# A hybrid decoder step on one core: part of the weight residuals computed on GpSimd, with seven part buffers and five raw buffers

## The chip, the cores and the metric

The kernel runs on one core of a Trainium2 chip. The metric is the device time of one execution in microseconds (us); several executions are timed and the median is given. A core has TensorE (PE in the profile, its weight loads PEld), VectorE (DVE), ScalarE (ACT), GpSimd (POOL) and SyncE (SP, which here only issues the loads of the weights).

## The reference: what is computed

One decoder layer on 264 tokens (256 of a new sequence and 8 single-token samples), all in float32, cut to what matters here:

```
h = h + 0.5 * swiglu(rmsnorm(h), ffn1_gate, ffn1_up, ffn1_down)
h = h + mixing_block(rmsnorm(h), w_in, ..., w_out)     # mLSTM heads beside short gated convolutions
h = h + 0.5 * swiglu(rmsnorm(h), ffn2_gate, ffn2_up, ffn2_down)
y = rmsnorm(h)

def swiglu(x, wg, wu, wd):
    return (jax.nn.silu(x @ wg) * (x @ wu)) @ wd
```

The model width is 2048 and the feed-forward width 5504, so that gate, up and down are 2048 x 5504 matrices, twice. They are read once, and each of their 128x128 blocks meets all 264 tokens.

## The kernel before, in words

**Two parts for each number.** TensorE multiplies float16 here. Each float32 weight tile, scaled by sw = 2^14, is cut into a high part hi = f16(sw*w) and a low part lo = f16(sw*w - hi), and the activations likewise; a product is hi*xhi + hi*xlo + lo*xhi, three matmuls (`three`, L324 to L327).

**One weight tile's way.** `fetch` (L257) takes the next tile from a fixed list (`weight_plan`, L93). A tile is 128 partitions by up to 8 blocks of 128 columns, 512 KB: a quarter of a gate-and-up block's weights. It is loaded into a raw buffer (wraw, six of them, AHEAD + 1) by a transfer that SP issues (L264); ScalarE writes the high part into a part buffer (w, also six), in `high` (L243); VectorE writes the low part with one scalar_tensor_tensor, sw*raw - hi, in `low` (L251). `release` (L285) issues the low parts. While the flag lag is set, as it is in the feed-forward stages from the fourth (first layer) or second (second layer) block on, the low part of a tile is issued one fetch after its high part, so that it stands later in VectorE's row. A raw buffer is free again when the low part has been written, a part buffer when TensorE has used it.

**What sets the order.** The order on each engine is the order in which the code issues. `product` (L329) and `product_pair` (L364) fetch as long as fewer than AHEAD = 5 tiles are ready, so a tile's three instructions stand five tiles before its use, between the steps of whatever product is being issued then. `at` and `tick` (L310, L313) put the steps that follow a product (activation, joins) half a product or more behind it. Each engine works off its own row strictly in order and waits on semaphores.

**Two kinds of products.** A plain block of gate or up (`block`, L833) is two `product`s, gate and up, of 16 weight blocks each: four tiles. Some pairs of blocks go by `by_seven` (L815) instead: gate and up of one block are computed together by seven half-size products in place of eight. For that VectorE forms sums of weight parts (`weight_sums`, L299, four additions for two tiles, tiles named s), and afterwards joins three PSUM banks (`join`, L423, lines L430 to L440, tile y). In each feed-forward layer the blocks 0 to 21 make up the first half and 22 to 42 the second, each followed by the down products of that half. From block 7 on (first layer) or block 3 on (second layer) every second block goes by seven, up to 19 in the first half, and from 22 every second up to 40 in the second: 7, 10, 9 and 10 blocks in four stretches, with a plain block between any two. Blocks 20, 21, 41 and 42 are plain. In the down products of a half three to five of the eight pairs of output blocks go by seven.

**The steps around a plain block.** For the gate product: L840 multiplies the PSUM bank by the token's norm (tile ta), ScalarE takes a sum over a few tokens (L573, seen) and the SiLU (L843, tb). For up: L846 (tile tc), L789 (silu times up, tc), then high and low part of the activation (a, L243 and L251). For a block by seven: L430 on ScalarE, L433 to L440 and L821 on VectorE (y), L824 (SiLU, tb), L789 (y) and the parts a.

**GpSimd's work before.** In the feed-forward stages it has work only where h gets its final value: a square (L725) and a sum (L729) for each of the next norm's 16 blocks, and one addition near the start (L744).

Of the kernel before, what the change touches and what calls it, by code (L numbers as in the profile page):

```python
# [8 lines left out]
F32 = mybir.dt.float32  # L9
# [4 lines left out]
ALU = mybir.AluOpType  # L14
# [14 lines left out]
WK = 8  # L29
# [138 lines left out]
def step(ctx: ExitStack, tc: tile.TileContext, a: dict, shared, bad=None):  # L168
# [3 lines left out]
    half_size = bad is not None  # L172
    PART = F16 if half_size else F32R
    sw, sx, s3 = (SW, SX, S3) if half_size else (1.0, 1.0, 1.0)
    sa = SA if half_size else {"1": 1.0, "2": 1.0}
    AHEAD = 5 if half_size else 2
    queue = nc.gpsimd if half_size else nc.sync
    side = nc.gpsimd if half_size else nc.vector

# [3 lines left out]
    wpool = ctx.enter_context(tc.tile_pool(name="wpool", bufs=3))  # L183
# [56 lines left out]
    def high(dst, src, scale=1.0):  # L240

        if half_size or not isinstance(scale, float):
            nc.scalar.activation(dst, src, AF.Copy, scale=scale)  # L243
        else:
            nc.scalar.copy(dst, src)

    def low(dst, src, hi, scale=1.0):

        hi = hi if half_size else hi.bitcast(F32)
        if half_size or not isinstance(scale, float):  # L250
            nc.vector.scalar_tensor_tensor(  # L251
                dst, src, scale, hi, op0=ALU.mult, op1=ALU.subtract
            )
        else:
            nc.vector.tensor_tensor(dst, src, hi, op=ALU.subtract)

    def fetch():  # L257

        if not plan:
            return  # L260
        key, src, n, m, several = plan.pop(0)
        raw = wpool.tile([128, WK, 128], F32, tag="wraw", name="wraw", bufs=AHEAD + 1)[:, :n, :m]
        dst = raw.rearrange("p (f k) m -> p f k m", f=several) if several > 1 else raw
        nc.sync.dma_start(dst, src)  # L264
        parts = wpool.tile([128, 2, WK, 128], PART, tag="w", name="w", bufs=AHEAD + 1)
        hi, lo = parts[:, 0], parts[:, 1]
        pairs = [(raw, (hi, lo), slice(0, m))]
        if half_size and key == "gates":

            pairs = [(raw[:, :, 32 * g :], (hi, lo), slice(16 * g, 16 * g + 16)) for g in (0, 1)]  # L270
        lows = []
        for src, (h_, l_), cols in pairs:
            h_, l_ = h_[:, :n, cols], l_[:, :n, cols]
            src = src[:, :, : cols.stop - cols.start]
            high(h_, src, sw)
            lows.append((l_, src, h_, sw))
        release()
        held.append((lows, (key, hi, lo, n), parts))
        if not lag[0]:
            release()  # L280


    held, lag = [], [False]

    def release():  # L285
        for lows, tile_, parts in held:
            for x in lows:
                low(*x)
            ready.append(tile_)
            if tile_[0][1] in ("gu", "dd"):  # L290
                beside.append(parts)
                if len(beside) == 2:
                    sums.append(weight_sums(*beside, tile_[3] // 2))
                    beside.clear()
        held.clear()

    beside, sums, spool = [], [], [None]

    def weight_sums(one, other, n):  # L299

        s = spool[0].tile([128, 4, 2, WK // 2, 128], PART, tag="s", name="s", bufs=3)[:, :, :, :n]
        a_, b_, c_, d_ = (w[:, :, i : 2 * n : 2] for w in (one, other) for i in (0, 1))
        for out, x, y in ((0, c_, d_), (1, b_, d_), (2, s[:, 0], b_), (3, s[:, 2], a_)):
            nc.vector.tensor_tensor(s[:, out], x, y, op=ALU.add)  # L304
        return s
# [23 lines left out]
    def product(key, x, order, m=128):  # L329

        tick()
        ps = bank()[:m, :T]
        k, half = 0, 0.5
        while k < len(order):
            while plan and len(ready) + len(held) < AHEAD:
                fetch()
            got, hi, lo, n = ready.pop(0)
            assert got == key, (got, key)
            for i in range(n):
                three(  # L340
                    ps, hi[:, i, :m], lo[:, i, :m], x[order[k]], k == 0, k == len(order) - 1
                )
                k += 1
            if k < len(order) or lag[0]:
                fetch()
            tick(half)
            half = 0
        return ps
# [15 lines left out]
    def product_pair(key, x, forms, order):  # L364
# [12 lines left out]
        while k0 < count:  # L377
            tiles = []
            for _ in range(2):
                while plan and len(ready) + len(held) < AHEAD or not ready:  # L380
                    fetch()
                tiles.append(ready.pop(0))
                assert tiles[-1][0] == key, (tiles[-1][0], key)
# [63 lines left out]
    def product_beside(key, x):  # L447
# [3 lines left out]
        for k0 in range(0, KB, WK):  # L451
            while plan and len(ready) + len(held) < AHEAD:
                fetch()
# [14 lines left out]
    def products2(keys, x, order):  # L468
# [3 lines left out]
        while k < len(order):  # L472
            tick()
            for j, key in enumerate(keys):
                while plan and len(ready) + len(held) < AHEAD:
                    fetch()
# [1237 lines left out]
```

## Time and profile before

| what | value |
|---|---|
| three timed runs | 1808.15, 1808.59, 1811.59 us; median 1808.59 us |
| the profiled execution: its own time | 1812.5 us |
| its span, first to last instruction | 1810.7 us |
| TensorE busy, clock granted | 1784.7 us (99%), 0.996 |
| VectorE busy | 1572.0 us (87%) |
| ScalarE busy | 896.0 us (49%) |
| GpSimd busy | 145.9 us (8%) |
| low parts of weight tiles on VectorE (L251, tile w) | 692 instructions, 800.3 us |
| high parts of weight tiles on ScalarE (L243, tile w) | 692 instructions, 665.3 us |
| transfers, mean rate | 211 GB/s |

The page of the profile lists busy time, a picture of the span in 40 slices, the chain of work that ended last, and groups of instructions with the idle time before them and what ended it. A timeline row has the start, the duration (from the first start to the last end, where it stands for several instructions in a row), engine, line, operation, tiles and count; in square brackets stands the idle time ahead of it and what ended that. Durations of consecutive instructions of one engine overlap a little, since the next starts before the last writes of the one before have landed; so the distance of two starts is the better price. A table of windows gives, for a stretch of the span, each engine's busy time and count.

### The profile page before, as it was taken

How to read it: one execution, taken by the hardware profiler on the slowest of the kernel's cores; microseconds unless marked ns; L12 is line 12 of the kernel's file. 1: busy time of each engine (PE TensorE's matmuls, PEld its weight loads, DVE VectorE, ACT ScalarE, POOL GpSimd, SP SyncE). 2: the span in 40 equal slices, each digit the busy share in tenths (PEclk: the TensorE clock that was granted, in tenths of full speed). 3: DMA queues.
4: the chain of work that ended last, by engine and by line, in shares of the span. 5: the costliest groups of instructions: out<-in, count | busy, mean ns of one | idle time of the engine just before them, and what ended most of it. 6: DMA issues, size and time to landing. Idle time of an engine off the chain costs nothing.

```text
span 1810.7 us, 45495 instructions
## 1 busy us (share of the span) xinstructions
PE 1784.7 (99%) x19080; PEld 1595.9 (88%) x19080; DVE 1572.0 (87%) x2528; ACT 896.0 (49%) x1571; POOL 145.9 (8%) x200
## 2 busy tenths in 40 slices
PE   8999999999999999999999999999999999999997
PEld 7899889999898988888888888899989999898896
DVE  7889988999998998788888866999989999999895
ACT  7544444435445445576576744454454444444543
POOL 0000000000000222222121032000000000000131
PEclk9999999999999999999999999999999999999998
DMA  8656666666666556888787655666665656666663
GB/s 289 203 180 196 196 210 204 209 205 195 193 209 210 179 171 214 289 296 283 271 266 255 224 185 177 205 199 191 206 217 190 212 188 205 193 210 190 212 187 116
DMA packets 118518, 381.54 MB, mean 211 GB/s; under 512 B 14972, under 2 KB 24796, under 8 KB 118304
## 3 DMA queue, kind: packets, MB, share of 16 engines
q1 hardware_dynamic: 109104, 350.53, 60.2%
q0 software_dynamic: 8256, 27.57, 4.4%
q8 instruction: 151, 2.47, 0.5%
q10 hardware_dynamic: 944, 0.45, 0.1%
q14 instruction: 63, 0.52, 0.1%
HBM read 366.72 MB, written 11.78 MB: 209 GB/s over the span
## 4 chain that ended last, share of the span: by engine, by line
PE 74%; DVE 17%; ACT 4%; issue 3%; DMA 1%; SPq 0%; ACTq 0%; DVEq 0%
PE ps L327 17%; PE ps L325 17%; PE ps L326 17%; PE ps L390 8%; PE ps L374 7%; PE ps L375 7%; DVE w L251 6%; DVE s L304 5%; ACT w L243 3%; DMA wraw<-in_w1gu 1%; DVE g L362 1%; DVE a L251 1%; DVE y L821 1%; PE ps L682 0%; DVE y L434 0%
## 5 line engine op out<-in xcount | busy, mean ns | idle before, releaser
L251 DVE SCALAR_TENSOR_TENSOR w<-wraw,w 128x1024 f16<-128x1024 f32 (+3 forms) x692 | 800.3, 1182 | 100.2 <-ACT w L243 99.1
L243 ACT ACTIVATE w<-wraw 128x1024 f16<-128x1024 f32 (+3 forms) x692 | 665.3, 1007 | 150.3 <-issue 56.0
L327 PE MATMUL ps<-x,w 128*128 128x264 f16 x1536 | 424.9, 277 | 4.6 <-DVE w L251 4.6
L325 PE MATMUL ps<-x,w 128*128 128x264 f16 x1536 | 424.9, 277 | 0.0
L326 PE MATMUL ps<-x,w 128*128 128x264 f16 x1536 | 424.8, 277 | 0.0
L327 PEld LDWEIGHTS <-w 128*128 128x128 f16 x3372 | 330.2, 98 | 56.9 <-DVE w L251 8.5
L326 PEld LDWEIGHTS <-w 128*128 128x128 f16 x3372 | 330.2, 98 | 49.7
L325 PEld LDWEIGHTS <-w 128*128 128x128 f16 x3372 | 330.4, 98 | 48.4 <-issue 0.6
L325 PE MATMUL ps<-xm,w 128*128 128x264 f16 x896 | 247.4, 276 | 0.0
L326 PE MATMUL ps<-xm,w 128*128 128x264 f16 x896 | 247.4, 276 | 0.0
L327 PE MATMUL ps<-xm,w 128*128 128x264 f16 x896 | 247.4, 276 | 0.0
L390 PEld LDWEIGHTS <-w 128*128 128x128 f16 x1886 | 181.1, 98 | 27.0 <-ACT w L243 1.8
L374 PEld LDWEIGHTS <-s 128*128 128x128 f16 x1872 | 180.0, 96 | 2.3 <-DVE s L304 2.2
L375 PEld LDWEIGHTS <-s 128*128 128x128 f16 x1872 | 181.7, 97 | 0.0
L327 PE MATMUL ps<-a,w 128*128 128x264 f16 (+2 forms) x684 | 180.2, 269 | 1.4 <-DVE w L251 1.4
L325 PE MATMUL ps<-a,w 128*128 128x264 f16 (+2 forms) x684 | 180.2, 269 | 0.0
L326 PE MATMUL ps<-a,w 128*128 128x264 f16 (+2 forms) x684 | 180.2, 269 | 0.0
L304 DVE TENSOR_TENSOR s<-s,w 128x1024 f16<-128x1024 f16 (+2 forms) x246 | 164.8, 670 | 4.3
L304 DVE TENSOR_TENSOR s<-w 128x1024 f16<-128x1024 f16 (+2 forms) x246 | 156.5, 677 | 5.3
L390 PE MATMUL ps<-x,w 128*128 128x264 f16 x1152 | 141.8, 276 | 1.1 <-ACT w L243 1.1
L375 PEld LDWEIGHTS <-w 128*128 128x128 f16 x1418 | 138.3, 98 | 2.5 <-DVE w L251 0.4
L374 PEld LDWEIGHTS <-w 128*128 128x128 f16 x1418 | 138.1, 97 | 2.0
(273 smaller groups left out, 2296.8 us busy)
## 6 DMA issues: line engine op xcount, KB each, us to landing
wraw<-in_w2gu SPq DMA_DIRECT2D x172, 512.0 KB, 4.7
wraw<-in_w1gu SPq DMA_DIRECT2D x164, 512.0 KB, 4.5
wraw<-in_win SPq DMA_DIRECT2D x112, 512.0 KB, 5.4
wraw<-in_w1d SPq DMA_DIRECT2D x42, 512.0 KB, 4.5
wraw<-in_w2d SPq DMA_DIRECT2D x38, 512.0 KB, 4.4
wraw<-in_w2d SPq DMA_DIRECT2D x42, 448.0 KB, 4.2
wraw<-in_wout SPq DMA_DIRECT2D x32, 512.0 KB, 4.4
wraw<-in_w1d SPq DMA_DIRECT2D x36, 448.0 KB, 4.0
```

What stands on the lines that cost most here:

```text
L243: nc.scalar.activation(dst, src, AF.Copy, scale=scale)
L251: nc.vector.scalar_tensor_tensor(dst, src, scale, hi, op0=ALU.mult, op1=ALU.subtract)
L304: nc.vector.tensor_tensor(s[:, out], x, y, op=ALU.add)
L325: nc.tensor.matmul(ps, wh, xk[:, 0, :], start=first, stop=False)
L326: nc.tensor.matmul(ps, wh, xk[:, 1, :], start=False, stop=False)
L327: nc.tensor.matmul(ps, wl, xk[:, 0, :], start=False, stop=last)
L362: nc.vector.tensor_tensor(out[:, n], a_, b_, op=op)
L374: nc.tensor.matmul(ps, w[0], x[:, 1], start=first, stop=False)
L375: nc.tensor.matmul(ps, w[1], x[:, 0], start=False, stop=last)
L390: nc.tensor.matmul(ps[:, :T], hi[:, i], xs[i][:, 0], start=(k0 + i == 0), stop=False)
L821: nc.vector.tensor_tensor(z, z, norm.r.unsqueeze(1).to_broadcast([128, 2, T]), op=ALU.mult)
```

## The change

It has two parts.

**Buffers.** AHEAD goes from 5 to 6. With AHEAD + 1 part buffers there are seven, and tiles are fetched one tile earlier in the row. The raw buffers go from AHEAD + 1 = 6 to AHEAD - 1 = 5.

**Low parts on GpSimd.** The tiles of plain gate and up products and of plain down products of the first half are counted, and every second one is `apart`: ScalarE first writes the high part as before, then scales the raw tile in place (a second activation, raw times sw, float32 to float32), and the low part is a tensor_tensor subtraction on GpSimd, raw - hi, in place of VectorE's scalar_tensor_tensor. This concerns 114 of 692 tiles, 102 of 128x1024 and 12 of 128x896. In a plain gate-and-up block it is the second tile of gate and the second of up; in the down products of the first halves 18 tiles in all.

```diff
-    AHEAD = 5 if half_size else 2
+    AHEAD = 6 if half_size else 2
...
-        raw = wpool.tile([128, WK, 128], F32, tag="wraw", name="wraw", bufs=AHEAD + 1)[:, :n, :m]
+        raw = wpool.tile([128, WK, 128], F32, tag="wraw", name="wraw", bufs=AHEAD + (-1 if half_size else 1))[:, :n, :m]
...
+        apart = half_size and len(key) > 2 and (key[1] in ("g", "u") or key[1:3] == ("d", 0))
+        turn[0] += apart
+        apart = apart and turn[0] % 2 == 0
         for src, (h_, l_), cols in pairs:
...
             high(h_, src, sw)
+            if apart:
+                high(src, src, sw)
             lows.append((l_, src, h_, sw))
         release()
-        held.append((lows, (key, hi, lo, n), parts))
+        held.append((lows, (key, hi, lo, n), parts, apart))
...
-        for lows, tile_, parts in held:
+        for lows, tile_, parts, apart in held:
             for x in lows:
-                low(*x)
+                if apart:
+                    side.tensor_tensor(*x[:3], op=ALU.subtract)
+                else:
+                    low(*x)
```

Here `side` is GpSimd. In the changed kernel all lines below are eight further down (L433 becomes L441, L789 L797, L846 L854), and GpSimd's low part is L294.

What this does to the rows of two engines is shown at one place, the stretch of blocks 22 to 42 of the first layer, from the up product of a plain block to the next join. On VectorE before, tc is up's activation, a the activation's parts, w a weight tile's parts and wraw its raw buffer, y5 the join:

```order
L846 TENSOR_TENSOR tc_7710<-ps_7646,rstd_663 128x264 [waits PE_49]
L789 TENSOR_TENSOR tc_7710<-tc_7710,tb_7642 128x264 [waits DVE_49]
L251 SCALAR_TENSOR_TENSOR w_7702<-wraw_7700,w_7702 128x1024 [waits DMAHW7_49,Activation_49]
L251 SCALAR_TENSOR_TENSOR w_7721<-wraw_7719,w_7721 128x1024 [waits DMAHW0_49,Activation_49]
L251 SCALAR_TENSOR_TENSOR a1_7000<-y5_7563,a1_7000 128x264
L251 SCALAR_TENSOR_TENSOR a1_7000<-tc_7710,a1_7000 128x264 [waits DVE_49]
L251 SCALAR_TENSOR_TENSOR w_7742<-wraw_7740,w_7742 128x1024 [waits DMAHW1_49,Activation_49]
L251 SCALAR_TENSOR_TENSOR w_7805<-wraw_7803,w_7805 128x1024 [waits DMAHW2_49,Activation_49]
L433 TENSOR_TENSOR y5_7885<-y5_7885,ps_7718 128x132 [waits Activation_49]
```

The same piece of VectorE's row in the changed kernel:

```order
L251 SCALAR_TENSOR_TENSOR w_7727<-wraw_7725,w_7727 128x1024 [waits DMAHW7_49,Activation_49]
L854 TENSOR_TENSOR tc_7765<-ps_7700,rstd_672 128x264 [waits PE_49]
L797 TENSOR_TENSOR tc_7765<-tc_7765,tb_7696 128x264 [waits DVE_49]
L251 SCALAR_TENSOR_TENSOR w_7776<-wraw_7774,w_7776 128x1024 [waits DMAHW1_49,Activation_49]
L251 SCALAR_TENSOR_TENSOR a1_7050<-y5_7617,a1_7050 128x264
L251 SCALAR_TENSOR_TENSOR a1_7050<-tc_7765,a1_7050 128x264 [waits DVE_49]
L251 SCALAR_TENSOR_TENSOR w_7861<-wraw_7859,w_7861 128x1024 [waits DMAHW3_49,Activation_49]
L441 TENSOR_TENSOR y5_7941<-y5_7941,ps_7773 128x132 [waits Activation_49]
```

Between tc's second step and the next join there stood four low parts of weight tiles; now there are two, and one low part has moved ahead of the up step. Tiles w_7761 and w_7797, which lie between, are GpSimd's.

ScalarE's row for the same place before, from the high part of up's activation (a) to the copy that starts the join:

```order
L243 ACTIVATE a1_7000<-tc_7710 128x264 [waits DVE_49]
L573 ACTIVATE seen_7714,stat_172<-ps_7646 128x16
L243 ACTIVATE w_7721<-wraw_7719 128x1024 [waits DMAHW0_49,PE_49]
L243 ACTIVATE w_7742<-wraw_7740 128x1024 [waits DMAHW1_49,PE_49]
L243 ACTIVATE w_7805<-wraw_7803 128x1024 [waits DMAHW2_49,PE_49,Activation_49]
L243 ACTIVATE w_7826<-wraw_7824 128x1024 [waits DMAHW3_49,PE_49,Activation_49]
L430 COPY y5_7885<-ps_7716 128x132 [waits DVE_49,PE_49,Activation_49]
```

And in the changed kernel, starting two tiles earlier:

```order
L243 ACTIVATE w_7727<-wraw_7725 128x1024 [waits DMAHW7_49,PE_49,Pool_49]
L243 ACTIVATE w_7761<-wraw_7759 128x1024 [waits DMAHW0_49,PE_49]
L243 ACTIVATE wraw_7759<-wraw_7759 128x1024 [waits Activation_49]
L243 ACTIVATE a1_7050<-tc_7765 128x264 [waits DVE_49]
L581 ACTIVATE seen_7769,stat_172<-ps_7700 128x16
L243 ACTIVATE w_7776<-wraw_7774 128x1024 [waits DMAHW1_49,PE_49,Pool_49]
L243 ACTIVATE w_7797<-wraw_7795 128x1024 [waits DMAHW2_49,PE_49]
L243 ACTIVATE wraw_7795<-wraw_7795 128x1024 [waits Activation_49]
L243 ACTIVATE w_7861<-wraw_7859 128x1024 [waits DMAHW3_49,PE_49]
L243 ACTIVATE w_7882<-wraw_7880 128x1024 [waits DMAHW4_49,PE_49]
L438 COPY y5_7941<-ps_7771 128x132 [waits DVE_49,PE_49]
```

The two steps that write wraw are the added scalings; the second stands between the high part of w_7776 and that of w_7861, both of which VectorE waits for.

More of the change, by code (lines that the diff above doesn't have):

```diff
@@ L295, in release @@
         held.clear()
-    beside, sums, spool = [], [], [None]
+    beside, sums, spool, turn = [], [], [None], [0]
     def weight_sums(one, other, n):
```

## The prediction

> **What bounds the kernel now.** I read the table of windows first, for where TensorE waits. Behind a window's name stand its length and then, for PE, PEld, DVE and ACT, the busy time.
>
> ```profile
> 100.00:222.00 122.00, 122.00 (x1408) 111.03 (x1407) 113.07 (x172) 53.37 (x94) 0.00 (x0) 1.00 0.61 191
> 222.00:226.00 4.00, 3.74 (x43) 3.13 (x41) 3.54 (x6) 3.68 (x7) 0.00 (x0) 1.00 0.42 143
> 472.00:476.00 4.00, 3.52 (x41) 2.96 (x39) 3.50 (x6) 3.39 (x7) 0.00 (x0) 1.00 0.38 118
> 550.00:562.00 12.00, 10.29 (x134) 9.01 (x132) 10.97 (x17) 6.59 (x13) 0.00 (x0) 1.00 0.51 173
> 1325.00:1330.00 5.00, 3.83 (x48) 3.17 (x46) 4.47 (x8) 2.81 (x6) 0.00 (x0) 1.00 0.48 134
> 1576.00:1580.00 4.00, 3.44 (x48) 3.00 (x46) 3.48 (x5) 2.44 (x6) 0.00 (x0) 1.00 0.46 140
> 1655.00:1666.00 11.00, 9.30 (x125) 8.13 (x123) 9.97 (x15) 5.65 (x12) 0.00 (x0) 1.00 0.54 157
> 300.00:380.00 80.00, 80.00 (x1015) 74.20 (x1013) 74.37 (x115) 31.64 (x41) 0.00 (x0) 1.00 0.64 204
> ```
>
> TensorE is the bound: in 100 to 222 it is never idle. It waits in six places, at the ends of the four stretches in which plain blocks and blocks by seven alternate and in the middle of two of them: 0.26 + 0.48 + 1.71 + 1.17 + 0.56 + 1.70 = 5.9 us. So the lead of the weight parts over TensorE is used up at the end of each stretch. VectorE is busy 113.07 of 122 us, and the question is whether its row is a second bound. The timeline of one period (a block by seven, a plain block) in blocks 22 to 42 of the first layer tells. VectorE, then ScalarE, then TensorE's first matmul of two consecutive blocks by seven:
>
> ```profile
> 478.27 0.29 DVE L433 TENSOR_TENSOR y<-y,ps 128x132 f32<-128x132 f32 x1
> ...
> 480.92 1.22 DVE L251 SCALAR_TENSOR_TENSOR w<-wraw,w 128x1024 f16<-128x1024 f32 x1
> 482.50 1.23 DVE L251 SCALAR_TENSOR_TENSOR w<-wraw,w 128x1024 f16<-128x1024 f32 x1 [0.36 <-ACT w L243]
> 483.76 1.29 DVE L304 TENSOR_TENSOR s<-w 128x1024 f16<-128x1024 f16 x2
> ...
> 486.30 0.43 DVE L840 TENSOR_TENSOR ta<-ps,rstd 128x264 f32<-128x264 f32 x1
> ...
> 486.98 1.22 DVE L251 SCALAR_TENSOR_TENSOR w<-wraw,w 128x1024 f16<-128x1024 f32 x1
> 488.63 1.23 DVE L251 SCALAR_TENSOR_TENSOR w<-wraw,w 128x1024 f16<-128x1024 f32 x1 [0.43 <-ACT w L243]
> ...
> 492.44 0.43 DVE L846 TENSOR_TENSOR tc<-ps,rstd 128x264 f32<-128x264 f32 x1
> 492.90 0.43 DVE L789 TENSOR_TENSOR tc<-tc,tb 128x264 f32<-128x264 f32 x1
> ...
> 494.93 1.23 DVE L251 SCALAR_TENSOR_TENSOR w<-wraw,w 128x1024 f16<-128x1024 f32 x1 [0.46 <-ACT w L243]
> 496.07 0.43 DVE L251 SCALAR_TENSOR_TENSOR a<-y,a 128x264 f16<-128x264 f32 x1
> ...
> 496.75 2.35 DVE L251 SCALAR_TENSOR_TENSOR w<-wraw,w 128x1024 f16<-128x1024 f32 x2
> 499.02 0.29 DVE L433 TENSOR_TENSOR y<-y,ps 128x132 f32<-128x132 f32 x1
> ```
> ```profile
> 486.76 0.18 ACT L573 ACTIVATE seen<-ps 128x16 f32<-128x16 f32 x1 [3.35 <-DVE ta L840]
> ...
> 487.56 1.99 ACT L243 ACTIVATE w<-wraw 128x1024 f16<-128x1024 f32 x2
> 493.36 0.42 ACT L243 ACTIVATE a<-tc 128x264 f16<-128x264 f32 x1 [3.81 <-DVE tc L789]
> ...
> 493.85 3.88 ACT L243 ACTIVATE w<-wraw 128x1024 f16<-128x1024 f32 x4
> ```
> ```profile
> 484.35 0.28 PE L390 MATMUL ps<-x,w 128*128 128x264 f16 x1
> ...
> 505.19 0.28 PE L390 MATMUL ps<-x,w 128*128 128x264 f16 x1
> ```
>
> TensorE's period is 20.84 us. VectorE never waits for TensorE here, but three times for ScalarE (0.36, 0.43, 0.46 us), and ScalarE in its turn for VectorE (3.35 and 3.81 us): the two form one closed loop. Its period is 499.02 - 478.27 = 20.75 us. So loop and TensorE are nearly level, and whatever lengthens the loop by more than 0.09 us comes out in the time.
>
> **What GpSimd costs VectorE.** The few GpSimd additions of before tell, where they meet VectorE. First the addition L729 (264 elements a partition) with VectorE's row beside it, then L744 (528 elements), then L729 beside steps that read PSUM:
>
> ```profile
> 618.59 1.61 POOL L729 TENSOR_TENSOR acc<-acc,sq 128x264 f32<-128x264 f32 x1
> ```
> ```profile
> 617.95 1.64 DVE L251 SCALAR_TENSOR_TENSOR w<-wraw,w 128x1024 f16<-128x1024 f32 x1
> 619.62 1.12 DVE L304 TENSOR_TENSOR s<-w 128x1024 f16<-128x1024 f16 x1
> ```
> ```profile
> 37.19 1.22 DVE L251 SCALAR_TENSOR_TENSOR w<-wraw,w 128x1024 f16<-128x1024 f32 x1
> 38.00 1.57 POOL L744 TENSOR_TENSOR sq<-sq 128x528 f32<-128x528 f32 x1 [34.21 <-ACT sq L737]
> 38.49 1.66 DVE L746 TENSOR_TENSOR sq<-sq,sq 128x528 f32<-128x528 f32 x1
> ```
> ```profile
> 628.72 0.90 POOL L729 TENSOR_TENSOR acc<-acc,sq 128x264 f32<-128x264 f32 x1
> ```
> ```profile
> 628.93 0.77 DVE L601 TENSOR_REDUCE downs<-ps 128x1 f32<-128x264 f32 x2
> ```
>
> L729 begins at 618.59, but VectorE's low part runs until 619.59, and only 0.60 us after that L729 ends; the sum L304 that VectorE starts at 619.62 takes 1.12 us instead of half of 1.29. L744 likewise ends 1.16 us after the low part of 37.19 has ended at 38.41, and VectorE's next step is held up. They exclude each other, instruction by instruction, when both read two operands from SBUF; steps that read PSUM run on (two in 0.77 us beside L729). From 0.60 us for 264 elements to 1.16 for 528 is 2.1 ns an element; for 1024 that gives 1.16 + 496 x 0.0021 = 2.2 us. I take a hold h = 2.17 us. No row has a subtraction with float16 operands: if bytes set the pace (6 read where 8 were) it is 0.75 of that, 1.63 us; if the conversion costs a quarter more, 2.7.
>
> The Trainium skill, "SBUF — State Buffer", section "Who interferes with whom", has this as a lock: a VectorE instruction with two SBUF inputs and a GpSimd instruction that reads SBUF share an interface, and the loser blocks for the whole instruction. That speaks against this change, and the rows agree. The Trainium skill's "GPSIMD Engine Reference", section 3.1, has 4497 ns for an addition of 2048 float32 elements; half, 2.25 us, is an estimate, and by it the main term below would be 5 us more.
>
> **The changed loop, step by step.** I walk through one period in the new order, with the distances of starts above, from the join's first step at 0. VectorE: first low part 2.65; since sums follow on it, 1.26 later (482.50 to 483.76) they begin, 3.91; four take 2.54 (to 486.30), 6.45; low part, 1.14 (494.93 to 496.07), 7.59; L848 and L797 0.34 each, 8.27; low part 9.53; sums 12.07; low part 13.21; L854 0.46, 13.67; then L797. ScalarE: it sees L848's end at 8.05, its next high part starts 0.80 later (486.76 to 487.56), 8.85, the second 0.95 after, the first GpSimd tile's, ready at 10.84, its scaling at 11.92. No row has this activation (1024, float32 to float32); the high part's 1.04 us is the nearest, and if twice as long it only delays the second GpSimd step. GpSimd then asks at about 12.1, just behind VectorE's low part, gets its turn at 13.21 and holds it for h, to 15.38. L854 reads PSUM and runs beside it; L797 is held from 13.67 to 15.38 and ends at 15.81. ScalarE waits for that: a at 15.84, high parts 16.33 and 17.28, second scaling 18.36 to 19.40, high part 19.31 to 20.35. VectorE: low part 17.40 (1.59 after L797's end, since the high part it needs stands behind a), two parts of a, 19.22 ready, waits for ScalarE until 20.38, but the second GpSimd step holds from 19.6 to 21.77; low part to 22.91, and the join begins again. The period is 22.91, in general 18.57 + 2h for h above 0.8, as h enters twice; without any hold, since neither step then waits, it would be 19.81. What is removed, two low parts of 1.14 us, is less than what GpSimd keeps from VectorE, 4.3 us.
>
> **The sum**, against the profiled execution's 1812.5 us:
> - The loop grows by 22.91 - 20.75 = 2.16 us. The stretches have 7, 10, 9 and 10 periods, less half of one each, since two plain blocks follow in which the loop catches up: 34 x 2.16 = +73.4. As the lead is used up at the end already, this falls on TensorE in full.
> - But one more tile is ahead, 20.84 / 8 = 2.6 us of TensorE's time. I count 2.1 of it, since a GpSimd tile's low part comes later behind its high part, and once per stretch, as it is used up like the rest: 4 x -2.1 = -8.4.
> - First-half down products: VectorE is free for 5.6 of 80 us there (last window), about 8 of 112; nine tiles add about 1.0 us each, 9. That is just covered, or costs 0 to 6 us; I take 3 in each layer: +6.
> - The other 24 tiles lie in plain blocks in a row, each about half of 20.84 us of TensorE's time for some 4 us of VectorE's steps (two low parts of 1.14, five of 0.3 to 0.5) and 4.3 us held: covered, +1 for the crowded starts. GpSimd's own work meets none of this: its squares lie in the second-half down products, which keep all their low parts on VectorE, but for L744 (below).
> - ScalarE's 114 scalings, 119 us, lie in its idle half except where the walk has them.
> - Raw buffers:
>
> ```profile
> wraw<-in_w2gu SPq DMA_DIRECT2D x172, 512.0 KB, 4.7
> ```
>
> A load waits until the low part of the tile five before is written. In the period that is over 7 us before ScalarE wants it, against 4.7: covered.
> - The start. ScalarE's row, then TensorE's wait for the first norm's sum of squares:
>
> ```profile
> 32.72 1.06 ACT L243 ACTIVATE w<-wraw 128x1024 f16<-128x1024 f32 x1 [2.04 <-DMA wraw<-in_w1gu]
> 33.68 2.23 ACT L737 ACTIVATE sq<-h 128x528 f32<-128x528 f32 x4
> ```
> ```profile
> 41.91 0.69 PE L682 MATMUL ps<-sq,ones 128*128 128x264 f32 x2 [2.68 <-DVE sq L748]
> ```
>
> Five tiles of 128x1024 stand ahead of these squares; now there are six, with three scalings among them and GpSimd's three low parts ahead of L744. ScalarE's idle time there (2.04 us in front of one tile) takes some of the 4 x 1.04 us. TensorE already waits, so what is left falls on it: 1 to 4 us, I take +2.5. The rest of the opening has one raw buffer less, which I count in that.
>
> Together +74.5, 1887.0 us for such an execution. The profiled one lies 3.9 us above the median, so I predict **1883 us**. With h = 1.63 the period is 21.83, the main term 36.7 and the time about 1846; with 2.7 it is 23.97, 109.5 and 1919.
>
> **Rivals.**
> - *VectorE is relieved and TensorE no longer waits* (the other side). If GpSimd's subtraction holds VectorE for well under 1.1 us, the loop falls below 20.84 (18.57 + 2h = 20.84 at h = 1.13), the 5.9 us of waits go and the 2.5 at the start stay: 1805, or 1803 if the start costs little. For it: GpSimd is idle in these stretches, and some of VectorE's steps (most of the join, L848, L854) read PSUM. Against it: 1.16 us for half the elements. 0.11.
> - *No difference:* h close to 1.1, or GpSimd's turns fall into VectorE's waits for ScalarE, so that loop and TensorE stay level: 1808. 0.04.
> - *The raw buffers bind as well:* the load of a GpSimd tile's successor starts only after its late low part; if landing takes 7 us in place of 4.7, ScalarE waits some 1 us a period: 34 us more, 1917. 0.07.
> - The forecast, the loop with h from 1.3 to 2.7: 0.78.
>
> **How the numbers follow.** A measurement tells 0.2%, about 3.6 us, here. Slower: 0.78 + 0.07 = 0.85; the first rival lies about that far below, so 0.08 of it is faster and 0.03, with the second's 0.04, is within: 0.07. The range leaves out the cases of the first two rivals and some of the tails: low 1824 (h about 1.35), high 1922.
>
> **What would show it.** Right: VectorE's joins in blocks 22 to 40 about 22.9 us apart, low parts or L797 drawn out by 1 us and more beside GpSimd steps of 2 us and more, TensorE waiting for low parts once in most periods, mostly by 2 us, and VectorE's busy time up though it does less. Wrong: GpSimd's step near 1 us, TensorE still never idle in 100 to 222, or VectorE's steps at their old length beside GpSimd; or TensorE waits while VectorE is idle, which would point to transfers or ScalarE.

## The result, and the profile after

| | before | after |
|---|---|---|
| median of the timed runs | 1808.72 us (6 runs) | 1888.83 us (6 runs, 1887.34 to 1891.94) |
| profiled execution: time, span | 1812.5, 1810.7 us | 1891.94, 1890.1 us |
| clock granted to TensorE | 0.996 | 0.989 |

The change makes the kernel slower by the ratio 1.0441, 95% interval 1.043 to 1.0453: 80 us between the medians, 79.4 between the two profiled spans. Forecast were 1883 us and a range of 1824 to 1922.

The chain that ended last, and three groups of instructions, from the page of the changed kernel (busy us and mean ns of one, then idle time ahead and what ended it):

```profile
DVE 44%; PE 40%; issue 7%; ACT 6%; DMA 2%; POOL 0%; SPq 0%; DVEq 0%; ACTq 0%
...
L251 DVE SCALAR_TENSOR_TENSOR w<-wraw,w 128x1024 f16<-128x1024 f32 (+5 forms) x578 | 776.6, 1364 | 165.6 <-ACT w L243 165.4
...
L335 PE MATMUL ps<-x,w 128*128 128x264 f16 x1536 | 429.0, 279 | 45.3 <-DVE w L251 43.6
L294 POOL TENSOR_TENSOR w<-wraw,w 128x1024 f16<-128x1024 f32 (+1 forms) x114 | 254.8, 2235 | 950.2 <-ACT wraw L243 901.9
```

VectorE writes 578 low parts where it wrote 692 in 800.3 us, but needs 776.6 us for them: one now takes 1364 ns. The chain has passed from TensorE (74% before, VectorE 17%) to VectorE. From the list of TensorE's waits (us in total, times, longest), it waits for low parts that VectorE writes, and hardly for GpSimd's:

```profile
PE ps L335 <- DVE w L251: 44.8, 28, 2.2
...
PE ps L335 <- POOL w L294: 1.4, 1, 1.4
```

One period in the same stretch as in the prediction. TensorE's first matmul of two consecutive blocks by seven, then GpSimd, VectorE and ScalarE:

```profile
558.70 0.50 PE L398 MATMUL ps<-x,w 128*128 128x264 f16 x3
```
```profile
581.50 0.61 PE L398 MATMUL ps<-x,w 128*128 128x264 f16 x4
```
```profile
522.04 2.13 POOL L294 TENSOR_TENSOR w<-wraw,w 128x1024 f16<-128x1024 f32 x1 [12.98 <-ACT wraw L243]
529.73 2.14 POOL L294 TENSOR_TENSOR w<-wraw,w 128x1024 f16<-128x1024 f32 x1 [5.57 <-ACT wraw L243]
544.85 2.13 POOL L294 TENSOR_TENSOR w<-wraw,w 128x1024 f16<-128x1024 f32 x1 [12.98 <-ACT wraw L243]
```
```profile
520.77 1.41 DVE L312 TENSOR_TENSOR s<-s,w 128x1024 f16<-128x1024 f16 x2
522.10 3.15 DVE L251 SCALAR_TENSOR_TENSOR w<-wraw,w 128x1024 f16<-128x1024 f32 x1
525.17 0.42 DVE L854 TENSOR_TENSOR tc<-ps,rstd 128x264 f32<-128x264 f32 x1
...
527.65 1.22 DVE L251 SCALAR_TENSOR_TENSOR w<-wraw,w 128x1024 f16<-128x1024 f32 x1 [1.60 <-ACT w L243]
...
530.64 2.32 DVE L251 SCALAR_TENSOR_TENSOR w<-wraw,w 128x1024 f16<-128x1024 f32 x1 [1.07 <-ACT w L243]
532.88 0.28 DVE L441 TENSOR_TENSOR y<-y,ps 128x132 f32<-128x132 f32 x1
```

GpSimd's step takes 2.13 us. The first begins at 522.04, just ahead of VectorE's low part at 522.10, which takes 3.15 us in place of 1.22: VectorE stands still until 524.17. The second, from 529.73 to 531.87, draws the low part at 530.64 out to 2.32 us. TensorE's period is 22.80 us where it was 20.84.

Both programs issue the same 19080 matmuls in the same order, so the n-th of one can be held against the n-th of the other; the growth of the distance of their starts shows where the 79.4 us arise:

| part | later by, us | forecast, us |
|---|---|---|
| start, to the first norm's sum of squares | +7.0 | +2.5 |
| the four stretches (7, 10, 9, 10 blocks by seven) | +16.6, +13.2, +21.2, +14.8 = +65.8 | 73.4 - 8.4 = +65.0 |
| down products, first halves | 0 | +6 |
| down products, second halves | +0.5 | no term |
| start of the mixing stage | +5.9 | no term |
| plain runs and mixing stage | +0.1 | +1 |

**The start.** ScalarE, then VectorE, with the squares (sq) on which the first norm waits:

```profile
36.98 1.06 ACT L243 ACTIVATE wraw<-wraw 128x1024 f32<-128x1024 f32 x1
37.94 2.23 ACT L745 ACTIVATE sq<-h 128x528 f32<-128x528 f32 x4
```
```profile
36.03 2.31 DVE L251 SCALAR_TENSOR_TENSOR w<-wraw,w 128x1024 f16<-128x1024 f32 x1 [1.63 <-ACT w L243]
39.14 3.40 DVE L754 TENSOR_TENSOR sq<-sq 128x528 f32<-128x528 f32 x3 [0.79 <-ACT sq L745]
42.45 2.33 DVE L251 SCALAR_TENSOR_TENSOR w<-wraw,w 128x1024 f16<-128x1024 f32 x1
44.70 3.35 DVE L754 TENSOR_TENSOR sq<-sq,sq 128x528 f32<-128x528 f32 x2
```

The squares begin at 37.94 where they began at 33.68, and VectorE's sums of them, two-operand steps, are held up as well: three in 3.40 us and two in 3.35, which took 2.33 and 2.47 before.

**The start of the mixing stage.** VectorE, with the last down product's step L903, then ScalarE:

```profile
730.59 4.46 DVE L251 SCALAR_TENSOR_TENSOR w<-wraw,w 128x1024 f16<-128x1024 f32 x3
734.97 0.42 DVE L903 SCALAR_TENSOR_TENSOR h<-ps,h 128x264 f32<-128x264 f32 x1
```
```profile
732.73 1.06 ACT L243 ACTIVATE w<-wraw 128x1024 f16<-128x1024 f32 x1 [1.03 <-DMA wraw<-in_win]
```

L903 gives the last block of h, for which the mixing stage waits. One more tile ahead means one more large low part in front of it, and that tile's load has not landed yet.

### The profile page after: what moved, and what is told of

The parts are those of the page before. It is cut to its first block, busy times and chain, and to the rows that moved or that the text cites. A ratio compares the mean times of both kernels' runs of the same rounds, so it can differ in the third digit from the quotient of the medians.

```text
span 1890.1 us, 45504 instructions
## 1 busy us (share of the span) xinstructions
PE 1810.6 (96%) x19080; PEld 1600.4 (85%) x19080; DVE 1597.2 (85%) x2414; ACT 1011.3 (54%) x1685; POOL 399.0 (21%) x314
## 3 DMA queue, kind: packets, MB, share of 16 engines
q8 instruction: 151, 2.47, 0.5%
## 4 chain that ended last, share of the span: by engine, by line
DVE 44%; PE 40%; issue 7%; ACT 6%; DMA 2%; POOL 0%; SPq 0%; DVEq 0%; ACTq 0%
DVE w L251 21%; PE ps L335 11%; PE ps L333 11%; PE ps L334 11%; DVE s L312 10%; ACT w L243 5%; DVE g L370 2%; PE ps L398 2%; PE ps L382 1%; PE ps L383 1%; DVE tc L797 1%; DVE y L829 1%; DVE a L251 1%; DVE y L442 1%; DMA wraw<-in_w1gu 1%
## 5 line engine op out<-in xcount | busy, mean ns | idle before, releaser
L251 DVE SCALAR_TENSOR_TENSOR w<-wraw,w 128x1024 f16<-128x1024 f32 (+5 forms) x578 | 776.6, 1364 | 165.6 <-ACT w L243 165.4
L294 POOL TENSOR_TENSOR w<-wraw,w 128x1024 f16<-128x1024 f32 (+1 forms) x114 | 254.8, 2235 | 950.2 <-ACT wraw L243 901.9
L335 PEld LDWEIGHTS <-w 128*128 128x128 f16 x3372 | 332.0, 98 | 105.0 <-DVE w L251 53.6
L334 PEld LDWEIGHTS <-w 128*128 128x128 f16 x3372 | 332.0, 98 | 51.7 <-issue 0.3
L333 PEld LDWEIGHTS <-w 128*128 128x128 f16 x3372 | 332.4, 99 | 50.2 <-issue 0.8
L398 PEld LDWEIGHTS <-w 128*128 128x128 f16 x1886 | 181.4, 98 | 25.3
L383 PEld LDWEIGHTS <-w 128*128 128x128 f16 x1418 | 138.2, 98 | 6.8 <-DVE w L251 4.8
```

Source lines behind the costliest of these rows:

```text
L251: nc.vector.scalar_tensor_tensor(dst, src, scale, hi, op0=ALU.mult, op1=ALU.subtract)
L294: side.tensor_tensor(*x[:3], op=ALU.subtract)
L333: nc.tensor.matmul(ps, wh, xk[:, 0, :], start=first, stop=False)
L334: nc.tensor.matmul(ps, wh, xk[:, 1, :], start=False, stop=False)
L335: nc.tensor.matmul(ps, wl, xk[:, 0, :], start=False, stop=last)
L383: nc.tensor.matmul(ps, w[1], x[:, 0], start=False, stop=last)
```

## The experiments

Times are medians; ratios are to runs of the kernel before on the same chip. The mean loop is the distance of VectorE's joins over four periods in blocks 22 to 40 of the first layer, one of which has the sums of activations (tile g); the ordinary period, without such sums, is in brackets. TensorE's own is 20.84. Two joins of the kernel before with these sums between them lie 23.35 us apart:

```profile
434.18 0.28 DVE L433 TENSOR_TENSOR y<-y,ps 128x132 f32<-128x132 f32 x1
...
453.79 1.32 DVE L362 TENSOR_TENSOR g<-a 128x1056 f16<-128x1056 f16 x2
...
457.53 0.28 DVE L433 TENSOR_TENSOR y<-y,ps 128x132 f32<-128x132 f32 x1
```

| run | time, us | ratio, 95% interval | loop, us |
|---|---|---|---|
| before | 1808.7 | | 21.40 (20.75) |
| the change | 1888.8 | 1.0441 [1.043, 1.0453] | 23.41 (22.81) |
| 1 buffers alone | 1809.7 | 1.0 [0.9991, 1.0008] | 20.84 |
| 2 VectorE subtracts | 1810.6 | 1.0008 [0.9999, 1.0017] | 20.72 |
| 3 memset | 1810.9 | 1.0011 [1.0002, 1.002] | 20.84 |
| 4 subtracted twice | 2018.9 (one execution) | | 25.36 (24.27) |
| 5 six ahead in the stretches only | 1805.3 | 0.9982 [0.9973, 0.9991] | 20.84 |
| 6 GpSimd alone, buffers of before | 1867.1 | 1.0325 [1.0309, 1.0341] | 22.73 (21.82) |
| 7 copy | 1811.2 (one execution) | | 21.19 (20.50) |
| 8 one tile of four | 1826.0 | 1.0098 [1.0082, 1.0113] | 22.35 (21.70) |
| 9 memset, buffers of before | 1819.6 | 1.0063 [1.0046, 1.008] | 21.96 (21.81) |
| 10 no scaling | 1884.3 | 1.0423 [1.0405, 1.044] | 23.05 (22.38) |
| 11 no scaling, buffers of before | 1808.8 | 1.0002 [0.9992, 1.0011] | 20.99 (19.85) |
| 12 as 5, six raw buffers | 1800.3 | 0.9952 [0.9939, 0.9966] | 20.84 |

The theory: GpSimd's subtraction shuts out VectorE's steps that read two operands from SBUF, for its whole length. The rivals: the raw buffers, ScalarE's scalings, or the new order of the rows.

### 1. The buffers alone

```diff
-        apart = apart and turn[0] % 2 == 0
+        apart = False
```

> The buffers of the changed kernel (AHEAD 6, seven part buffers, five raw ones), but no tile is apart: every low part is VectorE's and ScalarE scales nothing. Theory (GpSimd's subtractions exclude VectorE's two-operand steps, and that is the loss): the loop is that of before, 20.8 us, one tile more lead takes part of the 5.9 us of waits away, and the 3.5 us at the start of the mixing stage stay, since there a low part of the extra tile stands ahead of the last down step: 1803 to 1813 us. Rival (five raw buffers make the loads late): TensorE waits behind transfers in most periods, 1840 us or more.

Measured 1809.7 us. Matmul by matmul, with the cuts of the table above, TensorE loses 3.4 us at the start and 4.6 at the start of the mixing stage, and gains 7.8 in the stretches and 0.6 in the second-half down products (run 5's expectation cuts the last two elsewhere). So the buffers are not the loss, but they bring half of what is lost at the start and most of what is lost at the mixing stage, which the forecast had at nothing. Each of these is one execution. At the start, runs 1, 2, 3 and 7 lose 2.8 to 3.9 us; at the mixing stage the eight kernels with six tiles ahead there lose 1.9 to 6.0, so how the change's 5.9 us divide is not settled.

### 2 and 3. The same rows without GpSimd's hold

```diff
-                    side.tensor_tensor(*x[:3], op=ALU.subtract)
+                    nc.vector.tensor_tensor(*x[:3], op=ALU.subtract)
```

> All as in the changed kernel, buffers, order and ScalarE's scalings, but the subtraction of the 114 tiles is issued on VectorE, raw - hi, at the same place. Theory (exclusion): two more steps of 1.2 us on VectorE in each period but no hold of 2.13; the period falls from 22.8 to between 20.84 and 22.0 us, as the scalings still stand between high parts that VectorE waits for; 1808 to 1845 us, about 1820. Rival (ScalarE's scalings and the new order make the loss): the period stays above 22.3, 1870 us or more.

```diff
-                    side.tensor_tensor(*x[:3], op=ALU.subtract)
+                    side.memset(x[0], 0.0)
```

> The changed kernel with GpSimd's subtraction replaced by a memset of the same low part on GpSimd, which reads nothing from SBUF: the low parts of the 114 tiles are left out of the products. Order, scalings and waits stay. Theory (exclusion needs GpSimd to read SBUF): VectorE's low parts take 1.22 us again, the period is TensorE's 20.84, and only the start of the mixing stage and some 3 us at the start stay: 1806 to 1818 us. Rival (exclusion also with a GpSimd step that only writes, or the loss comes of low parts that arrive late in the new order): period 21.8 or more, above 1845 us.

Measured 1810.6 and 1810.9 us. VectorE's low parts (x instructions, busy us, mean ns) in the first stretch, from the groups by line: in the changed kernel, 115 to 231 us; then in run 2, with its subtractions, and in run 3, both 112 to 222 us:

```profile
L251 DVE SCALAR_TENSOR_TENSOR w<-wraw,w 128x1024 f16<-128x1024 f32 x30 | 49.5, 1651 | 11.2 <-ACT w L243 11.2
```
```profile
L251 DVE SCALAR_TENSOR_TENSOR w<-wraw,w 128x1024 f16<-128x1024 f32 x31 | 37.8, 1218 | 2.3 <-ACT w L243 2.3
...
L294 DVE TENSOR_TENSOR w<-wraw,w 128x1024 f16<-128x1024 f32 x11 | 13.4, 1222 | 0.6
```
```profile
L251 DVE SCALAR_TENSOR_TENSOR w<-wraw,w 128x1024 f16<-128x1024 f32 x32 | 39.0, 1219 | 12.8 <-ACT w L243 12.8
```

With a GpSimd step that only writes, VectorE's low part is back at 1219 ns from 1651, and 78 of the 80 us are gone though scalings and order stand as in the change. It is not that the memsets miss VectorE's steps: 63 of its 128x1024 low parts run beside one, by 0.1 us or more, and take 1218 ns in the mean. Over the whole execution, VectorE's steps beside one of these GpSimd steps are longer than their like in the kernel before by 159 us in the change, and by 0.6 with the memset. One thing besides the hold differs in run 3: most memsets do not wait for the scaling, so their tiles are ready earlier. Run 2 keeps that wait and is as fast. The scalings cost nothing in this order, even with all low parts on VectorE. Both rivals fall for the changed kernel.

### 4. The subtraction twice

```diff
                     side.tensor_tensor(*x[:3], op=ALU.subtract)
+                    side.tensor_tensor(*x[:3], op=ALU.subtract)
```

> GpSimd issues each of its 114 subtractions twice. Theory (each step of GpSimd holds VectorE for its whole length, twice a period): the period goes from 22.80 to about 22.8 + 2 x 2.13 = 27.1 us, 34 x 4.26 = 145 us more; the plain runs and first-half down products, where the single hold was just covered, add 30 to 60: 2050 to 2110 us. Rival (what counts is a fixed delay before GpSimd starts, or GpSimd's step runs mostly beside VectorE): under 1960 us.

Measured 2018.9 us: 130 more than the change, below what was expected. In the stretches the doubled holds add 89 us, not 145 (the ordinary period is 24.27, not 27.1); the first-half down products take 21 more and the plain runs 12. GpSimd and VectorE, one place of the trace:

```profile
1630.64 2.47 POOL L295 TENSOR_TENSOR w<-wraw,w 128x1024 f16<-128x1024 f32 x1
1633.07 2.58 POOL L294 TENSOR_TENSOR w<-wraw,w 128x1024 f16<-128x1024 f32 x1
```
```profile
1631.03 5.16 DVE L313 TENSOR_TENSOR s<-s,w 128x1024 f16<-128x1024 f16 x2
1636.11 3.14 DVE L251 SCALAR_TENSOR_TENSOR w<-wraw,w 128x1024 f16<-128x1024 f32 x1
```

Where both have steps queued they take turns, and VectorE's two sums take 5.16 us in place of 1.41. But a longer row of GpSimd also reaches into the join and into VectorE's waits, where it holds up nothing: in the period up to 512.14 us the second step of the second pair begins at 511.22 and lies beside the join, whose steps keep their 0.28 and 0.43 us. So not each microsecond of GpSimd is one of VectorE.

### 5. Six ahead in the stretches only

Here `few` is true at the start, false from the block on in which lag is set, and true again from the last three pairs of down products of the first layer through the mixing stage. The other places that compare with AHEAD are changed alike.

```diff
+        apart = False
...
-            while plan and len(ready) + len(held) < AHEAD:
+            while plan and len(ready) + len(held) < AHEAD - few[0]:
...
-            if k < len(order) or lag[0]:
+            if (k < len(order) or lag[0]) and len(ready) + len(held) < AHEAD - few[0]:
```

> No tile is apart; seven part and five raw buffers as in the changed kernel, but six tiles are kept ahead only where blocks by seven and plain blocks alternate and in the down products; at the start, and from the last three pairs of down products of the first layer through the mixing stage, it is five as in the kernel before. Theory (with the buffers alone, TensorE lost 3.4 us at the start and 5.2 at the start of the mixing stage because the sixth tile's steps stand ahead of the squares and of the last down step, and gained 7.8 in the stretches and 1.4 in the down products): both losses go, but for up to 1.5 us for the missing raw buffer, and the gains stay: 1800 to 1805 us. Rival (the losses come from five raw buffers in place of six): 1807 to 1811 us.

Measured 1805.3 us, at the edge of what was expected: faster than the kernel before. By the matmuls 0.5 us stay lost at the start and 2.4 at the mixing stage, in place of 3.4 and 4.6; the second lies within the scatter named under run 1, the first does not. The raw buffer was the next suspect (run 12).

### 6. GpSimd alone, with the buffers of before

```diff
-    AHEAD = 6 if half_size else 2
+    AHEAD = 5 if half_size else 2
...
-        raw = wpool.tile([128, WK, 128], F32, tag="wraw", name="wraw", bufs=AHEAD + (-1 if half_size else 1))[:, :n, :m]
+        raw = wpool.tile([128, WK, 128], F32, tag="wraw", name="wraw", bufs=AHEAD + 1)[:, :n, :m]
```

> The subtractions on GpSimd and the scalings on ScalarE alone, with the buffers of before: five tiles ahead, six part and six raw buffers. Theory (the subtractions alone carry the loss; the buffers take 9 us off in the stretches and add 9 at the two starts): 1884 to 1897 us. Rival (the loss needs both, late low parts and a raw buffer that comes free late): under 1865 us.

Measured 1867.1 us, a miss by 17 us at the least: nearer to the rival's bound. The timeline tells why. GpSimd, VectorE and ScalarE, one period:

```profile
448.18 2.13 POOL L294 TENSOR_TENSOR w<-wraw,w 128x1024 f16<-128x1024 f32 x1 [16.62 <-ACT wraw L243]
451.10 2.28 POOL L294 TENSOR_TENSOR w<-wraw,w 128x1024 f16<-128x1024 f32 x1 [0.80 <-ACT wraw L243]
```
```profile
449.02 2.36 DVE L251 SCALAR_TENSOR_TENSOR w<-wraw,w 128x1024 f16<-128x1024 f32 x1 [1.82 <-ACT w L243]
452.16 0.29 DVE L441 TENSOR_TENSOR y<-y,ps 128x132 f32<-128x132 f32 x1 [0.78 <-ACT y L438]
```
```profile
449.97 1.06 ACT L243 ACTIVATE wraw<-wraw 128x1024 f32<-128x1024 f32 x1
...
451.88 0.25 ACT L438 COPY y<-ps 128x132 f32<-128x132 f32 x1
```

With five tiles ahead, GpSimd's first step falls half into a wait of VectorE for ScalarE (its low part takes 2.36), the second beside the join, which reads PSUM and takes its usual time. So the sixth tile ahead had another effect than lead: it shifted GpSimd's steps beside VectorE's two-operand steps. The lead differs too: here, unlike in the change (1.4 us), TensorE waits most of all for GpSimd's own low parts (us in total, times, longest):

```profile
PE ps L335 <- POOL w L294: 25.6, 31, 0.9
```

What is left of the period looked like the scalings, as the join waits 0.78 us for ScalarE's copy behind them. Runs 9 to 11 test that.

### 7. A copy in place of the subtraction

```diff
-                    side.tensor_tensor(*x[:3], op=ALU.subtract)
+                    side.tensor_copy(x[0], x[2])
```

> GpSimd writes the low part of the 114 tiles as a copy of the high part, so that the products use the high part twice: it reads one operand from SBUF in place of two. Theory (any GpSimd step that reads SBUF excludes VectorE's two-operand steps): VectorE's low part beside a copy is drawn out by about the copy's own length, and the time lies between the memset's 1811 and the changed kernel's 1889, in proportion to the copy's length: about 1811 if it is under 1.1 us, about 1850 if it is 1.6. Rival (only a GpSimd step with two operands excludes): VectorE's low parts stay at 1.22 us and the time is 1808 to 1814 whatever the copy's length.

Measured 1811.2 us. VectorE and GpSimd:

```profile
516.63 1.27 DVE L251 SCALAR_TENSOR_TENSOR a<-y,a 128x264 f16<-128x264 f32 x1
517.82 0.42 DVE L251 SCALAR_TENSOR_TENSOR a<-tc,a 128x264 f16<-128x264 f32 x1
```
```profile
516.46 1.15 POOL L294 COPY w<-w 128x1024 f16<-128x1024 f16 x1 [5.06 <-ACT w L243]
```

A copy reads one operand and still shuts VectorE out: the step at 516.63 takes 1.27 us, its neighbour 0.42. That the time stays low is the copy's length: 1.15 us is about what a low part costs VectorE itself. So what counts is that GpSimd reads SBUF, and for how long. Length is not all that differs, though: the copy waits for the high part and not for the scaling, so it also begins earlier beside VectorE's row, and its place and its length are not told apart here.

### 8. One tile of four

```diff
-        apart = apart and turn[0] % 2 == 0
+        apart = apart and turn[0] % 4 == 0
```

> Every fourth of the counted tiles is apart in place of every second, 57 in all: of a plain gate-and-up block only the second tile of up. Buffers as in the changed kernel. Theory (each hold counts by itself, less what falls into VectorE's waits for ScalarE): one hold of 2.13 for one low part of 1.2 a period, 20.8 to 21.8 us against TensorE's 20.84; the start of the mixing stage keeps its 5 us, the start 4 to 6: 1812 to 1849 us, about 1825. Rival (the loss comes of the first hold alone, the second is free, or the reverse with no loss from one): 1870 us or more, or 1808 to 1812.

Measured 1826.0 us, as expected: half the holds cost 17 us, not 40, and 7 us of that lie at the two starts. The ordinary period is 21.70, but the lead of six tiles carries TensorE through most of each stretch: it runs at 20.84 but for three places, 480 us, 1254 to 1278 us and, by 1 us in all, 1333 to 1336 us.

### 9 to 11. Scalings and holds apart

```diff
-                    side.tensor_tensor(*x[:3], op=ALU.subtract)
+                    side.memset(x[0], 0.0)
```

with the buffers as in run 6:

> The buffers of before (five tiles ahead, six part and six raw buffers), ScalarE's scalings as in the change, and GpSimd's subtraction replaced by a memset: the low parts of the 114 tiles are left out of the products. With these buffers and the subtraction the period was 21.82 us. Theory (in that order both scalings stand in ScalarE's row between tc and the copy that starts the join, and VectorE's join waits 0.78 us for that copy, so that there the scalings bind and not the hold): the period stays near 21.8, 1855 to 1868 us. Rival (the hold binds there too): 20.84, 1806 to 1812 us.

Run 10 takes the scalings out of the change, run 11 out of run 6:

```diff
-            if apart:
-                high(src, src, sw)
```

> The changed kernel without ScalarE's 114 scalings: GpSimd subtracts the high part from the unscaled raw tile, so that the low parts of these tiles have a wrong value. Theory (both holds stay and fall on VectorE's two-operand steps, but one scaling of 1.0 us leaves ScalarE's row between tc and the join): the period goes from 22.8 to between 21.3 and 22.3 us, 1840 to 1875 us, about 1857. Rivals: the holds alone make the loss, 1883 to 1890 us; the scalings alone make it, 1806 to 1815 us.

> The same, GpSimd's subtraction without ScalarE's scalings, with the buffers of before. Theory (in that order one hold falls beside the join, which reads PSUM, and one mostly into a wait of VectorE for ScalarE, and the scalings made the loss): the period falls from 21.82 to between 20.84 and 21.3 us, 1806 to 1830 us. Rival (the holds make it): 21.8 or more, 1860 us or more.

Measured 1819.6, 1884.3 and 1808.8 us. Run 9 is half a hit: the ordinary period is 21.81, as in run 6, with VectorE's join waiting for ScalarE:

```profile
501.87 0.29 DVE L441 TENSOR_TENSOR y<-y,ps 128x132 f32<-128x132 f32 x1 [1.91 <-ACT y L438]
```

But the time is 48 us less than in run 6. The difference lies in the period with the sums of activations, two-operand steps of 0.7 us: without the hold it is 22.42, with it 25.49, so that the mean loop is 21.96 against 22.73. Over 36 periods that is an estimated 28 us. The rest goes with the lead: in run 6 TensorE waits 25.6 us for GpSimd's low parts, in run 9 never, as the memsets write them earlier. How the 48 us divide between the two is not shown. Run 10 is a miss the other way: in the changed order the holds alone make the loss, and without the scalings only 4.5 of the 80 us go. One VectorE and one GpSimd row from its timeline:

```profile
538.98 3.22 DVE L310 TENSOR_TENSOR s<-s,w 128x1024 f16<-128x1024 f16 x2
```
```profile
539.16 2.49 POOL L292 TENSOR_TENSOR w<-wraw,w 128x1024 f16<-128x1024 f32 x1 [12.58 <-ACT w L243]
```

The step starts earlier without the scaling and shuts out the two sums (3.22 us in place of 1.41) instead of the low part. Run 11 is a hit: with the old buffers and no scalings 114 subtractions on GpSimd cost no time. VectorE's join to join, then GpSimd's two steps, which together run until 416.29:

```profile
411.94 2.36 DVE L251 SCALAR_TENSOR_TENSOR w<-wraw,w 128x1024 f16<-128x1024 f32 x1 [0.72 <-ACT w L243]
414.22 0.28 DVE L439 TENSOR_TENSOR y<-y,ps 128x132 f32<-128x132 f32 x1
...
434.07 0.28 DVE L439 TENSOR_TENSOR y<-y,ps 128x132 f32<-128x132 f32 x1
```
```profile
411.04 5.25 POOL L292 TENSOR_TENSOR w<-wraw,w 128x1024 f16<-128x1024 f32 x2 [14.60 <-ACT w L243]
```

The first step lies in VectorE's wait and costs 1.14 us, the second beside the join: the ordinary period is 19.85, below TensorE's, and the mean loop 20.99. GpSimd is not free for VectorE here either: its steps beside GpSimd's are longer by 109 us in all, against 159 in the change, but that is less than the 137 us or so that these 114 low parts took on VectorE (1.22 us for each of 128x1024). The two costs are not additive with the old buffers: scalings 11 us, holds 0, both 59.

### 12. Six raw buffers as well

To run 5 this adds the sixth raw buffer; its room comes from the scaled gains, written over the unscaled ones.

```diff
-        raw = wpool.tile([128, WK, 128], F32, tag="wraw", name="wraw", bufs=AHEAD + (-1 if half_size else 1))[:, :n, :m]
+        raw = wpool.tile([128, WK, 128], F32, tag="wraw", name="wraw", bufs=AHEAD + (0 if half_size else 1))[:, :n, :m]
...
-        gains = const.tile([128, V_FIN], F32, name="gains")
+        gains = vecs[:, :V_FIN]
...
-                nc.vector.tensor_scalar_mul(gains, vecs[:, :V_FIN], sx)
+                nc.vector.tensor_scalar_mul(gains, gains, sx)
```

> The kernel with six tiles ahead only in the stretches and down products, and no tile apart, but with six raw buffers beside the seven part buffers; the room comes from the norm's scaled gains, which now overwrite the unscaled ones. Theory (what that kernel still lost at the two starts, 0.5 us at the first and 3.3 at the mixing stage by its trace, came from the fifth raw buffer): these go as well, 7.8 us less in the stretches and about 1 in the down products remain, 1798 to 1802 us. Rival (they come from the order of the steps or from the transfers' own speed): 1804 to 1807 us.

Measured 1800.3 us, ratio 0.9952 [0.9939, 0.9966]: as expected, faster than the kernel before by 8.5 us, and than the change by 88.6. No run has six raw buffers with six tiles ahead everywhere, so whether run 5's limit is still needed then stays open. From the list of TensorE's waits (us in total, times, longest):

```profile
PE ps L335 <- DVE w L251: 1.1, 3, 0.4
```

The waits for low parts, 5.9 us before and 44.8 in the changed kernel, are 1.1.

## Why the prediction was right, and where not

- **The hold.** Right: 2.13 us (forecast 2.17), extrapolated from additions of 264 and 528 elements. The Trainium skill's rule, in "SBUF — State Buffer", section "Who interferes with whom", agrees with runs 3 and 7: a GpSimd step that only writes leaves VectorE at 1219 ns, one that reads a single operand shuts it out.
- **The period.** 22.80 against 22.91 walked. One turn went the other way: GpSimd asked at 522.04, 0.06 us ahead of VectorE's low part and not just behind it, so the low part was held and not L797. The sum was the same, as the walk had VectorE stand still either way. But my sentence that GpSimd keeps 4.3 us a period from VectorE counted the whole of both holds. The drawn-out low parts show 1.93 and 1.10 us, as part of the second hold falls into a wait. VectorE's busy time grows by only 0.65 us a period, from 19.18 to 19.83; the rest is its waits for ScalarE, 1.60 + 1.07 in place of 1.25 us: the closed loop hands the delay round.
- **What the loop is.** The step "loop and TensorE are nearly level" took an ordinary period, 20.75. One in four also has the sums of activations and lasts 23.35, so VectorE's mean was 21.40, already above TensorE's 20.84, carried by the lead. That is where the 5.9 us of waits came from. The change brings 23.41.
- **The main term and the lead.** +65.0 forecast, +65.8 measured, but the agreement is partly luck. 9.7 us of it are half-clock time (below) that no term had, and without it the two second-half stretches cost 11.5 and 13.1 us each, not 18.4: TensorE still kept its 20.84 for four periods there, so the lead was worth more than the 2.1 us I counted. The first stretch went the other way, 15.0 us without the clock where the same count gives 11.9.
- **General form.** "h enters twice" (18.57 + 2h) held at 2.13, and its break-even of 1.13 us agrees with the copy of 1.15 (20.87 by the form, 20.50 measured), which costs nothing but also begins earlier than the form has it. It failed at twice the length: 24.27 against 27.1.
- **First-half down products.** 0 in place of +6: VectorE's free time covered nine holds in each, as the text's other end had it. Doubled, they cost 11.5 and 9.4 us.
- **The start.** +7.0 in place of +2.5. The step that failed counted four activations of 1.04 us on ScalarE, less its idle time, but not that VectorE's own sums of squares are two-operand steps and held up too. Run 1 puts 3.4 us on the buffers.
- **The mixing stage.** The step "covered" for the raw buffers looked at the period alone. At the start of the mixing stage the extra tile's low part stands in VectorE's row ahead of the last down step, and its load is late: 4.6 us in run 1; 5.9 in the change, 2.3 of it half clock.
- **Rivals.** Raw buffers that bind in the period: no (run 1; the loads land in 4.2 us, 4.7 before). VectorE relieved: no in the changed order, but run 11 shows that subtractions without the scalings cost no time where one of the two in a period lands beside the join. My sentence that GpSimd keeps more from VectorE than is removed holds for where this change puts the steps, not in general.

## What to carry to other kernels

Before work is moved to GpSimd, look at what VectorE does at the moment when that work will run: beside steps that read PSUM, or in VectorE's waits, it holds nothing up (of the 58 steps with PSUM beside a subtraction in the change, none is longer by more than 0.011 us); beside steps with two SBUF operands it can cost VectorE nearly its full length, here 1.93 of 2.13 us, where 1.22 was saved. A deeper prefetch also shifts every later instruction in each row: it can move a step out of a free place, or put a load ahead of the one step that the next stage waits for, so limit it to the stretches that need it. A loop's bound is its mean over all its kinds of periods, not the ordinary one.

## What the runs showed of the hardware

TensorE runs at half its clock for a while after some of its waits. In the table of windows of the changed kernel (busy us of PE, PEld, DVE, ACT, POOL, then the granted clock), around a place where the starts of two matmuls lie 2.48 us apart, up to 245.4:

```profile
240.00:244.00 4.00, 3.09 (x44) 2.31 (x41) 3.96 (x5) 2.02 (x3) 1.88 (x1) 1.00 0.62 209
244.00:248.00 4.00, 2.62 (x18) 2.10 (x19) 2.37 (x4) 1.83 (x5) 0.25 (x1) 0.84 0.66 159
248.00:252.00 4.00, 4.00 (x28) 3.08 (x26) 2.93 (x4) 3.88 (x5) 2.13 (x1) 0.73 0.70 229
252.00:256.00 4.00, 4.00 (x38) 3.48 (x36) 3.56 (x8) 1.14 (x3) 2.16 (x1) 1.00 0.72 211
```

From 246.75 to 250.05 the matmuls start 0.22 us apart in place of 0.11, which costs about 1.6 us. Six of the nine gaps of 2.48 us in the stretches were followed by such a piece of 3.0 to 3.4 us, none of the eleven of 2.07 us; with the two starts it is about 13.5 us in this execution against 1.7 before, so that about 12 of the 79.4 us are clock. The Trainium skill, "TensorE: Matmul & The Clock Gate", Part 1, has half rate after an idle window of about 3.4 us on a free-running grid; the length of the slow pieces agrees, but here gaps of 2.48 us were enough. A grid agrees too: the slow pieces that begin within running matmuls do so at 246.75, 502.73, 1298.02 and 1741.87 us, whole multiples of 3.4133 us apart but for 0.1. On that grid each of the six gaps had 2.06 us or more in one window, the other three at most 1.76. Gaps of 2.07 us that lay whole in a window had no slow piece behind them, so in this trace the limit lies close to 2.1 us.
